# Paired head products, interleaved quarters in the scan, and low parts of the mixer's weights on VectorE in a two-layer hybrid encoder

## The chip, the cores and the metric

One core of a Trainium2 chip runs the whole program. The metric is device microseconds of one execution, the median of three runs. Engine names are those of the profile: PE is TensorE, DVE is VectorE, ACT is ScalarE, POOL is GpSimd, SP issues the DMAs.

## The reference, cut to what matters

Two residual layers over 512 positions of 1024 channels, in float32. Each layer is a mixer (three token mixers side by side, gated and summed, then an output projection) and a feed-forward with a convolution.

```python
h = rms_norm(x, attn_norm[l])
(qa, ka, va, qs, ks_, vs, qkv_c, z_c, beta_c, a_c, gate_c) = jnp.split(h @ w_in[l], splits, axis=-1)
# n: neighbourhood attention, 4 heads; s: sliding window, 8 query heads on 2 key heads
# g: bidirectional gated delta net, 4 heads of 64, chunks of 64 positions, both directions:
lower = where(strict, (k*beta) @ k.T * decay, 0)      # per head and chunk, 64x64
u, w  = solve(lower + I, [v*beta, k*beta*exp(g)])
qk    = (q @ k.T) * decay
def step(S, xs):                                      # over the 8 chunks, one after the other
    v_new = u_c - w_c @ S
    o_c   = q_c @ S + qk_c @ v_new
    S     = S * d_c + k_c.T @ v_new
merged = g_na*(y_na @ w_branch_na[l]) + g_swa*(y_swa @ w_branch_swa[l]) + g_gdn*(y_gdn @ w_branch_gdn[l])
x = x + merged @ w_out[l]
u = depthwise_conv_centred(rms_norm(x, ffn_norm[l]) @ w_up[l], ffn_conv_w[l]) + ffn_conv_b[l]
a, b = jnp.split(u, 2, axis=-1)
x = x + (silu(a) * b) @ w_down[l]
```

## The kernel before, in words

Channels lie on the partitions and the 512 positions along a row, so a tile of activations is 128x512. All weights come as chunks of 1024x128 from one array, in a fixed numbering: 0 to 51 are projections, gates and branch weights of the mixer, 52 to 59 the output projection, 60 to 103 the up-projection (`CH_UP = 60`), 104 to 127 the down-projection. `load_w` fetches a chunk in halves of 128x512. A dense product in float32 is made of three products in a rounded format: ACT copies a half to its rounded high part (`wh`, line 142), POOL subtracts that from the raw half and writes the low part (`wl`, line 144), and `mm3` (lines 150 to 152) issues high x high, high x low and low x high, each 128x128 weights by 512 columns. There are three buffers each of raw, high and low halves, and six accumulators `mm` in PSUM. A layer has 256 halves, 120 of them in chunks below 60, and 3024 dense products.

The mixer is a list of steps (`ORDER`). Those of the delta net are, in turn: gates and projections (`gg`, `gp`), `gdn_cross` (products of keys with keys and queries for each head, with decays), `gdn_solve` (31 steps of elimination on DVE, lines 713 and 715, then transposes, lines 722 to 728, and small products on PE from line 749 on), `gdn_mid` (lines 783 to 815), `gdn_scan` (eight chunks, forward on partitions 0 to 63 and backward on 64 to 127) and `gdn_out` (from line 872). The delta net has three PSUM banks (`gd`). The attention steps `na` and `sa` (lines 415 to 540) and the gates of the merge lie beside them. In a step of the scan PE multiplies the state by `wn` (line 832), DVE adds the product to `VN` (835), PE multiplies `VN` by `kT` (843), DVE adds that to the decayed state `SA` (848).

A scheduler orders the instructions of each engine before the program runs, from its own estimate of times; each engine then works through its list strictly in turn and waits on semaphores. So a change of one line moves instructions all over the lists.

Of the kernel before, what the change touches and what calls it, by code (L numbers as in the profile page):

```python
# [7 lines left out]
F32 = mybir.dt.float32  # L8
# [27 lines left out]
CH_UP = 60  # L36
# [25 lines left out]
def encoder_kernel(ctx, tc, xT, wall, par, cst, nab, out, depth=2, dbg=None):  # L62
# [70 lines left out]
    def load_w(l, c, nk=8):  # L133
# [3 lines left out]
        for o in range(0, nk, 4):  # L137
# [6 lines left out]
            G.tensor_tensor(lo[:, :n], raw[:, :n], hi.bitcast(F32)[:, :n], op=ALU.subtract)  # L144
# [130 lines left out]
    for l in range(depth):  # L275
# [374 lines left out]
        def gdn_cross():  # L650
            line[0] = "g"
            nonlocal Q, Qu, Xo, Xg, Lt, Rt, kds, qdec

            Q, Qu = by2("Q")
            Xo, Xg, Lt = (big(F32, (128, 32, 32), name=n) for n in ("Xo", "Xg", "Lt"))
            kds = [[doubled(kq[j][i][:, :, 0, :]) for i in range(2)] for j in range(2)]
            qdec = pair(name="qd") + pair(name="qd")
            for hh in range(4):
                j, rr = hh // 2, slice(64 * (hh % 2), 64 * (hh % 2) + 64)
                pe, pr = decay_sums(hh, (msr, blk))  # L660
                eg = tmp(name="eg")
                S.activation(out=eg, in_=pr, func=AF.Exp)
                for d in range(2):
                    r = slice(64 * d, 64 * d + 64)
                    for i in range(2):
                        ns = slice(4 * i, 4 * i + 4)
                        V.tensor_tensor(n8(qdec[hh])[r, ns], n8(eg)[r, ns], kq[j][i][rr, :, 1, :], op=ALU.mult)  # L667
                T.matmul(pe, lhsT=idb, rhs=nmb.unsqueeze(1).to_broadcast([128, 8, 64]), start=False, stop=True)
                e = tmp(name="E")
                S.activation(out=e, in_=pe, func=AF.Exp)  # L670
                on("ebk", "V").tensor_tensor(n8(e), n8(e), bc(bk, hh, 0, 8), op=ALU.mult)
                xt = tmp(name="X")
                for n0 in (0, 4):
                    kd = kds[j][n0 // 4]
                    pk = bank("gd")
                    for n in range(4):
                        T.matmul(pk[:, 128 * n:128 * n + 128], lhsT=kd[rr, n].rearrange("p d i -> p (d i)"),
                                 rhs=kq[j][n0 // 4][rr, n].rearrange("p c i -> p (c i)"), start=True, stop=True)
                    pkv = pk.rearrange("p (n c i) -> p c n i", n=4, c=2)
                    en = n8(e)[:, n0:n0 + 4]  # L680
                    V.tensor_tensor(n8(xt)[:, n0:n0 + 4], pkv[:, 0], en, op=ALU.mult)
                    V.tensor_tensor(Qu[n0 // 4 * 2 + hh // 2][:, :, hh % 2], pkv[:, 1], en, op=ALU.mult)

                for q4 in range(4):
                    r = slice(32 * q4, 32 * q4 + 32)
                    o = 32 * (q4 % 2)
                    cpx = (S.activation if q4 % 2 else G.tensor_copy)(
                        out=Xg[r].rearrange("p i (h n) -> p h n i", h=4)[:, hh], in_=n8(xt)[r, :, o:o + 32], **({"func": AF.Copy} if q4 % 2 else {}))
                    if q4 == 2:
                        lastg[0] = cpx  # L690
                    if q4 in (0, 3):
                        S.activation(out=Xo[r, 8 * hh:8 * hh + 8], in_=n8(xt)[r, :, 32 - o:64 - o], func=AF.Copy)
            Rt = big(F32, (128, 32, 32), "Rt")
# [123 lines left out]
        def gdn_scan():  # L817
# [7 lines left out]
            for s in range(8):  # L825
                ns = (s, 7 - s)
                half = [slice(0, 64), slice(64, 128)]
                if s:
                    pv = bank("gd", (128, 4, 64))
                    for d, r in enumerate(half):  # L830
                        for hh in range(4):
# [4 lines left out]
                if s < 7:  # L836
                    pd = bank("gd", (128, 4, 64))
                    sd = tmp(shape=(128, 8, 64), name="sd")[:, 0:4]
                    for d, r in enumerate(half):
                        if s:  # L840
                            G.tensor_tensor(sd[r], SA(ns[d])[r], hn(dec[:, 64:96])[r, :, ns[d]].unsqueeze(2).to_broadcast([64, 4, 64]), op=ALU.mult)
                        for hh in range(4):
# [289 lines left out]
```

## Time and profile before

| | us |
|---|---|
| median of 3 runs | 1711.9 (1708.8 to 1712.89) |
| the profiled execution | 1711.75 |
| its span, first to last instruction | 1710.0 |
| mean granted TensorE clock, share of full | 0.986 |
| PE busy | 1656.6 |
| POOL in line 144 | 683.8 in 512 instructions |

The profile is read in stretches of time from the start of the span. In the first layer the mixer runs up to about 521 us, and the first product of the solve stands at 259 us; the feed-forward ends at about 895 us. The second layer repeats this from 895 us, with the first product of its solve at 1105 us and its feed-forward from about 1366 us. A busy PE in these rows can include products that only wait in the pipe, so the number of products in a stretch is read beside the busy time.

### The profile page before, as it was taken

The page shows a single profiled execution, that of the slowest core. Times are in us where ns is not written, and L with a number is a line of the kernel's source. Part 1 is how long each engine was busy: PE and PEld are TensorE (multiplying, and loading weights), DVE is VectorE, ACT ScalarE, POOL GpSimd, SP SyncE. Part 2 cuts the span into 40 slices and gives each one's busy share as a digit, 9 for nine tenths or more (in the row PEclk, how much of TensorE's full clock was granted, in tenths as well). Part 3 has the DMA queues.
Part 4 walks back from the last instruction along what each step waited for, and adds up shares of the span by engine and source line. Part 5 has one row for each costly group of instructions (what it writes and reads, how often), then busy time and mean ns, then how long its engine had stood idle before and what let it go on. Part 6 is the DMA issues. An engine that isn't in the chain of part 4 may idle for free.

```text
span 1710.0 us, 25217 instructions
## 1 busy us (share of the span) xinstructions
PE 1656.6 (97%) x9196; PEld 1319.6 (77%) x9196; DVE 1008.1 (59%) x1809; ACT 739.1 (43%) x1436; POOL 834.5 (49%) x752
## 2 busy tenths in 40 slices
PE   7989999999999999999999998899999999999999
PEld 5766767777888888878886776777878888888887
DVE  5489996534547777741125898955255487777200
ACT  5445545423445444443334555554234354444321
POOL 4665442264544555544448554422644545555543
PEclk9989999999999999999999999999999999999999
DMA  5222211122452332234333221110324523222432
GB/s 205 74 64 76 70 62 45 38 69 73 132 190 87 99 99 96 96 115 132 114 104 94 67 72 56 56 44 26 99 91 138 178 87 99 93 93 92 136 121 70
DMA packets 91500, 160.46 MB, mean 94 GB/s; under 512 B 10352, under 2 KB 17136, under 8 KB 91376
## 3 DMA queue, kind: packets, MB, share of 16 engines
q1 hardware_dynamic: 91376, 158.85, 28.9%
q8 instruction: 72, 1.18, 0.3%
q14 instruction: 52, 0.43, 0.1%
HBM read 147.80 MB, written 8.39 MB: 91 GB/s over the span
## 4 chain that ended last, share of the span: by engine, by line
PE 79%; DVE 14%; issue 3%; ACT 2%; DMA 1%; POOL 0%; SPq 0%; DVEq 0%; ACTq 0%; POOLq 0%
PE mm L152 23%; PE mm L150 23%; PE mm L151 23%; DVE Rt L715 1%; DVE Tm L713 1%; PE at L535 1%; PE at L531 1%; DVE qd L667 1%; DVE lg L428 1%; DVE fix L172 1%; PE gd L843 1%; PE gd L832 1%; DVE fix L170 1%; PE gd L812 1%; PE at L509 1%
## 5 line engine op out<-in xcount | busy, mean ns | idle before, releaser
L144 POOL TENSOR_TENSOR wl<-wr,wh 128x512 fp32r<-128x512 f32 (+1 forms) x512 | 683.8, 1344 | 792.2 <-ACT wh L142 739.1
L150 PE MATMUL mm<-hh,wh 128*128 128x512 f32 x1408 | 560.2, 398 | 15.3 <-ACT wh L142 13.1
L152 PE MATMUL mm<-hh,wl 128*128 128x512 f32 x1408 | 559.3, 399 | 1.8 <-POOL wl L144 1.7
L151 PE MATMUL mm<-hl,wh 128*128 128x512 f32 x1408 | 556.0, 395 | 0.1
L142 ACT ACTIVATE wh<-wr 128x512 fp32r<-128x512 f32 (+1 forms) x512 | 312.4, 617 | 354.7 <-PE mm L151 213.0
L150 PEld LDWEIGHTS mm<-hh,wh 128*128 128x128 f32 x1408 | 268.0, 190 | 74.2 <-ACT wh L142 15.9
L152 PEld LDWEIGHTS mm<-hh,wl 128*128 128x128 f32 x1408 | 267.7, 190 | 65.1 <-POOL wl L144 6.2
L151 PEld LDWEIGHTS mm<-hl,wh 128*128 128x128 f32 x1408 | 267.7, 190 | 58.3 <-issue 1.9
L234 DVE SCALAR_TENSOR_TENSOR cv<-up,fix,cv 128x511 f32<-128x511 f32 x88 | 142.0, 1613 | 2.8
L233 DVE SCALAR_TENSOR_TENSOR cv<-up,fix,cv 128x511 f32<-128x511 f32 x88 | 85.9, 977 | 88.5 <-ACT cv L232 88.5
L152 PE MATMUL mm<-act,wl 128*128 128x512 f32 x352 | 137.2, 390 | 0.6 <-POOL wl L144 0.6
L150 PE MATMUL mm<-act,wh 128*128 128x512 f32 x352 | 137.1, 389 | 0.3 <-ACT wh L142 0.3
L151 PE MATMUL mm<-act,wh 128*128 128x512 f32 x352 | 137.0, 389 | 0.0
L971 DVE TENSOR_TENSOR xo<-xo,mm 128x512 f32<-128x512 f32 x16 | 11.0, 687 | 192.3 <-PE mm L152 192.3
L232 ACT ACTIVATE cv<-up,fix 128x512 f32<-128x512 f32 x88 | 70.8, 809 | 34.7 <-DVE up L280 34.7
L162 ACT ACTIVATE act<-cv 128x512 fp32r<-128x512 f32 x44 | 27.8, 632 | 126.0 <-DVE cv L954 126.0
L152 PEld LDWEIGHTS mm<-act,wl 128*128 128x128 f32 x352 | 66.1, 188 | 15.3 <-POOL wl L144 1.3
L150 PEld LDWEIGHTS mm<-act,wh 128*128 128x128 f32 x352 | 66.1, 188 | 14.2 <-ACT wh L142 0.7
L151 PEld LDWEIGHTS mm<-act,wh 128*128 128x128 f32 x352 | 66.1, 188 | 13.7
L953 ACT ACTIVATE cv<-cv 128x512 f32<-128x512 f32 x44 | 27.8, 633 | 86.2 <-DVE cv L234 86.2
L280 DVE TENSOR_TENSOR up<-mm,rstd 128x512 f32<-128x512 f32 x88 | 59.5, 680 | 8.2 <-ACT rstd L228 8.2
L900 ACT ACTIVATE gt<-gt 128x512 f32<-128x512 f32 x48 | 30.2, 630 | 66.4 <-DVE gt L280 66.3
(285 smaller groups left out, 2228.5 us busy)
## 6 DMA issues: line engine op xcount, KB each, us to landing
wr<-in_wall_dram SPq DMA_DIRECT2D x496, 256.0 KB, 2.8
xs<-xo SPq DMA_DIRECT2D x24, 256.0 KB, 2.9
xo<-xs SPq DMA_DIRECT2D x24, 256.0 KB, 3.7
xo<-in_xT_dram SPq DMA_DIRECT2D x16, 256.0 KB, 4.9
sw<-raw SPq DMA_DIRECT2D x40, 64.0 KB, 2.0
wr<-in_wall_dram SPq DMA_DIRECT2D x16, 128.0 KB, 3.3
out_dram<-xo SPq DMA_DIRECT2D x8, 256.0 KB, 2.1
nab<-in_nab_dram SPq DMA_DIRECT2D x8, 248.0 KB, 2.8
```

The source lines that it names most:

```text
L142: S.activation(out=hi[:, :n], in_=raw[:, :n], func=AF.Copy)
L144: G.tensor_tensor(lo[:, :n], raw[:, :n], hi.bitcast(F32)[:, :n], op=ALU.subtract)
L150: T.matmul(acc, lhsT=wh, rhs=rh, start=start, stop=False)
L151: T.matmul(acc, lhsT=wh, rhs=rl, start=False, stop=False)
L152: T.matmul(acc, lhsT=wl, rhs=rh, start=False, stop=stop)
L162: S.activation(out=hi, in_=src, func=AF.Copy)
L232: S.activation(out=dst, in_=src, func=AF.Identity, scale=w[:, 1:2], bias=bias)
L233: V.scalar_tensor_tensor(dst[:, 1:L], src[:, 0:L - 1], w[:, 0:1], dst[:, 1:L], op0=ALU.mult, op1=ALU.add)
L234: V.scalar_tensor_tensor(dst[:, 0:L - 1], src[:, 1:L], w[:, 2:3], dst[:, 0:L - 1], op0=ALU.mult, op1=ALU.add)
L280: V.tensor_tensor(dst, acc, rstd, op=ALU.mult)
L900: S.activation(out=gt[q], in_=gt[q], func=AF.Tanh, scale=0.5)
L953: S.activation(out=cv[0], in_=cv[0], func=AF.Silu)
```

## The change: what it does

Three edits. Low parts of chunks below 60 (all weights in front of the feed-forward) are written by DVE instead of POOL. In `gdn_cross` two heads, which lie on partitions 0 to 63 and 64 to 127, go through the products of line 677 together, each into a bank of its own, and their products stand in turn; their copies follow after both. In `gdn_scan` the products stand in turn between the two directions, not four of one and then four of the other.

```diff
-            G.tensor_tensor(lo[:, :n], raw[:, :n], hi.bitcast(F32)[:, :n], op=ALU.subtract)
+            (G if c >= CH_UP else V).tensor_tensor(lo[:, :n], raw[:, :n], hi.bitcast(F32)[:, :n], op=ALU.subtract)
...
-            for hh in range(4):
-                j, rr = hh // 2, slice(64 * (hh % 2), 64 * (hh % 2) + 64)
+            for j in range(2):
+                es, xts = [], []
+                for e in range(2):
+                    hh, rr = 2 * j + e, slice(64 * e, 64 * e + 64)
...
                 for n0 in (0, 4):
                     kd = kds[j][n0 // 4]
-                    pk = bank("gd")
+                    pks = [bank("gd") for _ in range(2)]
                     for n in range(4):
-                        T.matmul(pk[:, 128 * n:128 * n + 128], lhsT=kd[rr, n].rearrange("p d i -> p (d i)"),
-                                 rhs=kq[j][n0 // 4][rr, n].rearrange("p c i -> p (c i)"), start=True, stop=True)
...
+                        for e in range(2):
+                            rr = slice(64 * e, 64 * e + 64)
+                            T.matmul(pks[e][:, 128 * n:128 * n + 128], lhsT=kd[rr, n].rearrange("p d i -> p (d i)"),
+                                     rhs=kq[j][n0 // 4][rr, n].rearrange("p c i -> p (c i)"), start=True, stop=True)
...
                     pv = bank("gd", (128, 4, 64))
-                    for d, r in enumerate(half):
-                        for hh in range(4):
+                    for hh in range(4):
+                        for d, r in enumerate(half):
                             T.matmul(pv[r, hh], lhsT=n8(wn[hh])[r, ns[d]], rhs=SA(ns[d])[r, hh], start=True, stop=True,
...
-                        for hh in range(4):
+                    for hh in range(4):
+                        for d, r in enumerate(half):
                             T.matmul(pd[r, hh], lhsT=kT(ns[d], hh)[r], rhs=VN(ns[d])[r, hh], start=True, stop=True,
```

Lines after the edits move by 6 to 10: 677 becomes 683, 713 and 715 become 722 and 724, 749 becomes 758, 832 becomes 841, 843 becomes 852. This text uses the numbers of before.

On PE, in the first step of the first layer's scan, the four products of the forward state stand before the four of the backward state:

```order
L832 MATMUL gd_2946<-SA_2928,wn_564_2736 64x64
L832 MATMUL gd_2946<-SA_2928,wn_565_2737 64x64
L832 MATMUL gd_2946<-SA_2928,wn_566_2738 64x64
L832 MATMUL gd_2946<-SA_2928,wn_567_2739 64x64
L832 MATMUL gd_2946<-SA_2931,wn_564_2736 64x64
L832 MATMUL gd_2946<-SA_2931,wn_565_2737 64x64
L832 MATMUL gd_2946<-SA_2931,wn_566_2738 64x64
L832 MATMUL gd_2946<-SA_2931,wn_567_2739 64x64
```

Now they stand in turn (`SA_2928` is the forward state, `SA_2931` the backward one):

```order
L841 MATMUL gd_2946<-SA_2928,wn_564_2736 64x64
L841 MATMUL gd_2946<-SA_2931,wn_564_2736 64x64
L841 MATMUL gd_2946<-SA_2928,wn_565_2737 64x64
L841 MATMUL gd_2946<-SA_2931,wn_565_2737 64x64
L841 MATMUL gd_2946<-SA_2928,wn_566_2738 64x64
L841 MATMUL gd_2946<-SA_2931,wn_566_2738 64x64
L841 MATMUL gd_2946<-SA_2928,wn_567_2739 64x64
L841 MATMUL gd_2946<-SA_2931,wn_567_2739 64x64
```

The eight products are the same; what moved is their turn.

On DVE, in the middle of the elimination of the first layer (`Tm` and `Rt` are its two instructions), there stood only work of the merge beside the chain:

```order
L713 TENSOR_TENSOR Tm_2424<-Lt_2158,Rt_2335 128x252
L715 TENSOR_TENSOR Rt_2335<-Rt_2335,Tm_2424 128x18x14
L713 TENSOR_TENSOR Tm_2424<-Lt_2158,Rt_2335 128x255
L715 TENSOR_TENSOR Rt_2335<-Rt_2335,Tm_2424 128x17x15
L912 SCALAR_TENSOR_TENSOR ma_651_3323<-gt_635_3243,mm_3337 128x512
L912 SCALAR_TENSOR_TENSOR ma_652_3324<-gt_636_3244,mm_3345 128x512
L713 TENSOR_TENSOR Tm_2424<-Lt_2158,Rt_2335 128x256
L912 SCALAR_TENSOR_TENSOR ma_677_3433<-gt_661_3353,mm_3435 128x512
L715 TENSOR_TENSOR Rt_2335<-Rt_2335,Tm_2424 128x16x16
```

Now low parts (`wl`) and instructions of the neighbourhood attention (lines 422 to 428) stand in it:

```order
L144 TENSOR_TENSOR wl_3457<-wr_3453,wh_3455 128x512
L722 TENSOR_TENSOR Tm_2424<-Lt_2158,Rt_2335 128x255
L422 ISA lg_1277,fix<-at_1284,nab_1275,fix 128x192
L422 ISA fix 128x1
L724 TENSOR_TENSOR Rt_2335<-Rt_2335,Tm_2424 128x17x15
L722 TENSOR_TENSOR Tm_2424<-Lt_2158,Rt_2335 128x256
L426 RECIPROCAL fix<-fix 128x2
L724 TENSOR_TENSOR Rt_2335<-Rt_2335,Tm_2424 128x16x16
L428 TENSOR_SCALAR lg_1277<-lg_1277,fix 128x192 x2
L722 TENSOR_TENSOR Tm_2424<-Lt_2158,Rt_2335 128x255
L724 TENSOR_TENSOR Rt_2335<-Rt_2335,Tm_2424 128x15x17
```

Ahead of the last transpose of the solve DVE has 61 low parts more than before in the first layer and 62 in the second; its other work ahead of that place is the same.

On PE, around the first product of the first layer's solve, sliding-window attention (lines 509 to 535) and branch products stood directly ahead of it, and both groups of 32 stood together:

```order
L535 MATMUL at_1751<-th_1766,sv_335 64x256 x2
L509 MATMUL at_1799<-kdh_61_284,qs_101_464 128x384
L510 MATMUL at_1799<-kdl_63_286,qs_101_464 128x384
L535 MATMUL at_1751<-th_1775,sv_335 64x256 x2
L509 MATMUL at_1804<-kdh_62_285,qs_102_465 128x384
L510 MATMUL at_1804<-kdl_64_287,qs_102_465 128x384
L749 MATMUL gd_2556<-WT_2525,Xo_2156 32x32 x32
L749 MATMUL gd_2591<-WT_2525,Xo_2156 32x32 x32
L152 MATMUL mm_3614<-hh_85,wl_3606 128x512
```

Now dense products of the gates stand ahead, and the groups are cut up:

```order
L152 MATMUL mm_3673<-hh_131,wl_3665 128x512
L150 MATMUL mm_3673<-hh_142,wh_3669 128x512
L151 MATMUL mm_3673<-hl_143,wh_3669 128x512
L531 MATMUL at_1752<-fix,spr_1736 128x128
L531 MATMUL at_1752<-fix,spr_1723 128x128
L531 MATMUL at_1752<-fix,spr_1741 128x128
L150 MATMUL mm_3712<-hh_85,wh_3702 128x512
L151 MATMUL mm_3712<-hl_86,wh_3702 128x512
L758 MATMUL gd_2556<-WT_2525,Xo_2156 32x32
L758 MATMUL gd_2591<-WT_2525,Xo_2156 32x32
L758 MATMUL gd_2556<-WT_2525,Xo_2156 32x32 x21
```

What moved: ahead of this product stand 736 dense products of the layer where 692 stood, with 8 products of line 531, 6 of line 535 and 8 of lines 509 and 510 fewer; in the second layer 758 where 692 stood, with the same attention. Between it and the scan stand 82 dense products in the first layer and 70 in the second where 126 stood, and in the scan 81 and 92 where 147 stood. Of the products of line 683 about half stand in turn; for the others the second bank comes free later and four of one head stand together.

## Rows read from the trace of the kernel before

**Rows 1.** The page, its parts 1, 2 and 4: shares, PE in forty slices, the chain by engine.

```profile
PE 1656.6 (97%) x9196; PEld 1319.6 (77%) x9196; DVE 1008.1 (59%) x1809; ACT 739.1 (43%) x1436; POOL 834.5 (49%) x752
...
PE   7989999999999999999999998899999999999999
...
PE 79%; DVE 14%; issue 3%; ACT 2%; DMA 1%; POOL 0%; SPq 0%; DVEq 0%; ACTq 0%; POOLq 0%
```

**Rows 2.** Busy time by stretch; each engine with its instructions, TensorE clock, DMA share, GB/s.

```profile
60.00:259.00 199.00, 180.20 (x950) 134.76 (x948) 175.14 (x380) 103.51 (x231) 113.39 (x138) 0.96 0.24 73
...
259.00:277.00 18.00, 17.97 (x307) 13.88 (x308) 9.92 (x35) 11.19 (x30) 2.94 (x3) 0.81 0.15 46
...
330.00:384.00 54.00, 53.88 (x402) 41.85 (x402) 21.86 (x54) 16.25 (x34) 32.80 (x34) 1.00 0.20 65
...
570.00:600.00 30.00, 30.00 (x134) 24.83 (x133) 21.26 (x23) 13.61 (x23) 15.77 (x12) 1.00 0.30 93
...
895.00:960.00 65.00, 57.91 (x307) 43.37 (x306) 42.64 (x86) 28.94 (x57) 45.05 (x34) 0.89 0.27 82
...
960.00:1105.00 145.00, 133.33 (x709) 102.04 (x707) 133.70 (x305) 80.06 (x186) 76.22 (x107) 0.99 0.20 64
...
1123.00:1176.00 53.00, 53.00 (x499) 40.63 (x498) 29.09 (x88) 27.23 (x71) 10.00 (x8) 1.00 0.11 36
```

**Rows 3.** Busy time by stretch, of line 144 (low parts on POOL) alone; same columns.

```profile
60.00:259.00 199.00, 57.80 (x43) 0.96 0.24 73
...
895.00:1105.00 210.00, 65.17 (x47) 0.96 0.22 70
```

**Rows 4.** Timeline of DVE, 217 to 226: start, duration, engine, line, operation, tiles, shape, count.

```profile
217.83 0.42 DVE L715 TENSOR_TENSOR Rt<-Rt,Tm 128x252 f32<-128x252 f32 x1
...
218.36 1.40 DVE L713 TENSOR_TENSOR Tm<-Lt,Rt 128x255 f32<-128x255 f32 x1
...
219.79 1.40 DVE L715 TENSOR_TENSOR Rt<-Rt,Tm 128x255 f32<-128x255 f32 x1
...
223.76 1.48 DVE L713 TENSOR_TENSOR Tm<-Lt,Rt 128x255 f32<-128x255 f32 x1
```

**Rows 5.** Timeline of POOL, the same stretch.

```profile
218.18 4.17 POOL L144 TENSOR_TENSOR wl<-wr,wh 128x512 fp32r<-128x512 f32 x3 [4.39 <-PE mm L152]
...
223.68 1.29 POOL L144 TENSOR_TENSOR wl<-wr,wh 128x512 fp32r<-128x512 f32 x1 [1.33 <-ACT wh L142]
```

**Rows 6.** Instructions of one line (163, then 234): durations in ns, least, median, most.

```profile
L163 DVE TENSOR_TENSOR act<-cv,act x44: 677/692/694, 533.1 to 1595.7; 128x512 fp32r<-128x512 f32 x44
...
L234 DVE SCALAR_TENSOR_TENSOR cv<-up,fix,cv x88: 737/1661/1777, 525.3 to 1592.6; 128x511 f32<-128x511 f32 x88
```

**Rows 7.** Timeline of PE in the scan: 343 to 346.

```profile
343.70 0.96 PE L832 MATMUL gd<-SA,wn 64*64 64x64 f32 x16
...
344.60 0.65 PE L535 MATMUL at<-th,sv 128*64 128x256 f32 x4
...
345.18 1.13 PE L843 MATMUL gd<-VN,kT 64*64 64x64 f32 x16
```

**Rows 8.** Timeline of PE in the middle step, 286 to 288.

```profile
286.72 1.38 PE L794 MATMUL gd<-W,kE 64*64 64x64 f32 x40
```

**Rows 9.** Timeline of PE in the head products, 1010 to 1012.

```profile
1010.40 1.16 PE L677 MATMUL gd<-kq,dup 64*128 64x128 f32 x8
...
1011.49 0.50 PE L150 MATMUL mm<-hh,wh 128*128 128x512 f32 x1
```

**Rows 10.** Timeline of PE, 246 to 264, up to the first solve product.

```profile
246.77 0.93 PE L531 MATMUL at<-fix,spr 128*128 128x128 f32 x7
...
259.03 3.81 PE L749 MATMUL gd<-WT,Xo 32*32 32x32 f32 x128 [2.72 <-DVE fix L513]
```

**Rows 11.** Groups of instructions by line: busy, mean ns, idle before and its releaser.

```profile
L835 DVE TENSOR_TENSOR VN<-gd,VN 64x256 f32<-64x256 f32 x28 | 11.8, 423 | 22.9 <-PE gd L832 22.5
...
L152 PE MATMUL mm<-hh,wl 128*128 128x512 f32 x1408 | 559.3, 399 | 1.8 <-POOL wl L144 1.7
```

More of the change, by code (lines that the diff above doesn't have):

```diff
@@ L657, in gdn_cross @@
             qdec = pair(name="qd") + pair(name="qd")
-            for hh in range(4):
-                j, rr = hh // 2, slice(64 * (hh % 2), 64 * (hh % 2) + 64)
[L660 to L672, printed above, removed]
+            for j in range(2):
+                es, xts = [], []
+                for e in range(2):
+                    hh, rr = 2 * j + e, slice(64 * e, 64 * e + 64)
+                    pe, pr = decay_sums(hh, (msr, blk))
+                    eg = tmp(name="eg")
+                    S.activation(out=eg, in_=pr, func=AF.Exp)
+                    for d in range(2):
+                        r = slice(64 * d, 64 * d + 64)
+                        for i in range(2):
+                            ns = slice(4 * i, 4 * i + 4)
+                            V.tensor_tensor(n8(qdec[hh])[r, ns], n8(eg)[r, ns], kq[j][i][rr, :, 1, :], op=ALU.mult)
+                    T.matmul(pe, lhsT=idb, rhs=nmb.unsqueeze(1).to_broadcast([128, 8, 64]), start=False, stop=True)
+                    ex = tmp(name="E")
+                    S.activation(out=ex, in_=pe, func=AF.Exp)
+                    on("ebk", "V").tensor_tensor(n8(ex), n8(ex), bc(bk, hh, 0, 8), op=ALU.mult)
+                    es.append(ex)
+                    xts.append(tmp(name="X"))
@@ L673, in gdn_cross @@
                 for n0 in (0, 4):
                     kd = kds[j][n0 // 4]
-                    pk = bank("gd")
+                    pks = [bank("gd") for _ in range(2)]
                     for n in range(4):
-                        T.matmul(pk[:, 128 * n:128 * n + 128], lhsT=kd[rr, n].rearrange("p d i -> p (d i)"),
-                                 rhs=kq[j][n0 // 4][rr, n].rearrange("p c i -> p (c i)"), start=True, stop=True)
-                    pkv = pk.rearrange("p (n c i) -> p c n i", n=4, c=2)
@@ L680, in gdn_cross @@
[L680 to L692, printed above, removed]
+                        for e in range(2):
+                            rr = slice(64 * e, 64 * e + 64)
+                            T.matmul(pks[e][:, 128 * n:128 * n + 128], lhsT=kd[rr, n].rearrange("p d i -> p (d i)"),
+                                     rhs=kq[j][n0 // 4][rr, n].rearrange("p c i -> p (c i)"), start=True, stop=True)
@@ new lines, in gdn_cross @@
+                    for e in range(2):
+                        pkv = pks[e].rearrange("p (n c i) -> p c n i", n=4, c=2)
+                        en = n8(es[e])[:, n0:n0 + 4]
+                        V.tensor_tensor(n8(xts[e])[:, n0:n0 + 4], pkv[:, 0], en, op=ALU.mult)
+                        V.tensor_tensor(Qu[n0 // 4 * 2 + j][:, :, e], pkv[:, 1], en, op=ALU.mult)
+                for e in range(2):
+                    hh = 2 * j + e
+                    for q4 in range(4):
+                        r = slice(32 * q4, 32 * q4 + 32)
+                        o = 32 * (q4 % 2)
+                        cpx = (S.activation if q4 % 2 else G.tensor_copy)(
+                            out=Xg[r].rearrange("p i (h n) -> p h n i", h=4)[:, hh], in_=n8(xts[e])[r, :, o:o + 32], **({"func": AF.Copy} if q4 % 2 else {}))
+                        if q4 == 2:
+                            lastg[0] = cpx
+                        if q4 in (0, 3):
+                            S.activation(out=Xo[r, 8 * hh:8 * hh + 8], in_=n8(xts[e])[r, :, 32 - o:64 - o], func=AF.Copy)
```

## The prediction

> **What bounds the kernel now.** First the page: PE is busy for 97% of the span and holds 79% of the chain that ended last, DVE holds 14% of it [rows 1]. So time is won by less work on PE, or where PE is short of work. The forty slices show where that is: PE falls to 8 or 9 tenths only near the start and around slice 22, where the layers begin [rows 1]. The stretches say it sharper [rows 2]. In the feed-forward 134 dense products go through in 30.0 us, 0.224 us each, with PE full; nothing in the change touches that. From 60 us to the solve of the first layer at 259 us PE is busy for 180.2 of 199 us at a clock of 0.96, while DVE is busy for 175.1. In the second layer, from 895 to 1105 us, PE misses 7.1 and 11.7 us, and from 960 us on DVE is busy for 133.7 of 145. So ahead of the solve DVE sets the pace, and PE has about 19 us of idle time in each layer besides a lower clock. The product that opens the solve came after 2.72 us of idle PE, released by DVE [rows 10]; behind it the granted clock of the stretch is 0.81, that is some time at the lower of its two levels (1.2 and 2.4 GHz) [rows 2]. From there to the end of the layer PE is full: 53.00 of 53 us ahead of the scan in the second layer, 53.88 of 54 in the first one's scan [rows 2]. The end of a layer is therefore the start of its solve plus the PE work behind that.
>
> **Scan in turn: 8.1 us less on PE.** Sixteen records (eight products, two passes each) of line 832 take 0.96 us, four products of one quarter at a time [rows 7]. Line 794 already stands in turn between the same two quarters: 40 records in 1.38 us, so with 0.22 us for the last one 1.16/39 = 0.030 us from one to the next [rows 8]. Sixteen then take 15 x 0.030 + 0.22 = 0.67 us, 0.29 us less; 14 batches in each of two layers give 28 x 0.29 = 8.1 us. But both halves now end together and DVE adds them one after the other (0.42 us each [rows 11]). The shortest half-step of before is 1.48 us from line 832 to 843, with 0.6 us of other work between [rows 7]. The new one can hardly be under 0.67 + 0.42 + 0.34 + 0.1, about 1.5 us. In the order of after five half-steps of a layer have between 0 and 1 us of other PE work between their batches, against four of 0.3 to 1.4 before; those five leave some 2 us of idle PE in a layer. I put back 4 us, with 0 and 12 as ends: the DVE queue has 7 or 8 low parts in a scan, and each can hold an add back by 0.7 us.
>
> **Head products in turn: nothing on the end.** Eight records of line 677 take 1.09 us to the next instruction [rows 9]. No row shows two tiles of 64 rows and 128 columns side by side: with nothing gained the 128 records cost what they do, with a full halving they would save 16 x 0.5 = 8 us, and since only half of them stand in turn in the order, 4 us. They stand ahead of the solve, where DVE sets the pace, so I count 0; the ends are -4 and +2 (a second bank of three is taken, and a head's decay sums wait for it).
>
> The Trainium skill (TensorEngine Tiling (Array Packing), Theoretical Speedup) gives up to twice the rate where the contraction has at most 64 rows. By it, as an estimate, the half that stands in turn would save those 4 us of PE work; the trace agrees for 64x64 quarters and shows nothing for 64x128, and the sum stays as it is.
>
> **Low parts on DVE: what they cost it.** 240 of 512 low parts move, 120 in a layer. An operation of this form with two inputs in SBUF takes 0.69 us on DVE [rows 6]. In 60 to 259 us 43 low parts ran on POOL, in 895 to 1105 us 47 [rows 3]; on DVE they are 43 x 0.69 = 30 us and 47 x 0.69 = 32 us. Against that stands what they cost DVE from POOL. Steps of the elimination take 0.42 us; the three that met a low part on POOL took 1.40, 1.40 and 1.48 us [rows 4, 5]. Four low parts there cost DVE 3.0 us, 0.76 each. The same is seen in the feed-forward, where line 234 has 0.74 us at least and 1.66 us in the middle [rows 6]. At 0.76 each 43 and 47 low parts give back 33 and 36 us. So the start of a solve lies between 4 us earlier (all low parts met such an operation) and 32 us later (none did). I take 0, nearest to the stretch that shows it; what is moved also has a cover in DVE's first 60 us and at 895 to 960 us, where DVE is busy for 42.6 of 65 [rows 2].
>
> The trace shows the two engines in each other's way there [rows 4, 5]. The Trainium skill (GPSIMD Engine Reference, Key points) has a rule for it that speaks against the change: GpSimd shares its interfaces to SBUF with VectorE, for VectorE operations with two SBUF inputs among others, and the new low parts are such operations. What that would do here is rival 4.
>
> **PE work moved ahead of the solve: 20 us.** With the solve at the same time, the 44 and 66 dense products that now stand ahead of it no longer stand behind it: 9.9 and 14.8 us at 0.224 us [rows 2]. In the first layer attention goes the other way: eight products of line 531 (16 records at 0.93/7 us [rows 10], 2.1 us), six of line 535 (0.65 us for four records [rows 7], 1.9 us), eight of 509 and 510 at some 0.15 us, together 5 us. Net 4.9 and 14.8 us. This fits into the 19 us that PE idles in front of each solve. The ends are 0 (PE idles behind the solve instead) and 20.
>
> **Two costs of the new order.** Behind the solve of the second layer 70 dense products fill the chain up to the scan where 126 did, 12.5 us less filler in 53 us that were full [rows 2]; I take 4 us of new idle time there, between 0 and 10. And a low part now waits in DVE's queue behind adds and evictions that wait for PE. Until now PE waited 1.7 us in all for low parts [rows 11]. In the order, most low parts have 6 to 10 us of PE work between the last product that DVE must wait for and their first use, but some 15 of 240 have under 2.7 us; at a quarter of a microsecond each that is 4 us, between 0 and 15. The output projection is covered: there a chunk's two low parts stand a whole chunk ahead.
>
> **Sum.** The profiled execution took 1711.75 us (span 1710.0 and 1.75 around it), the median of the runs is 1711.9, so no correction is needed. 1711.75 - 8.1 + 4 + 0 + 0 - 19.7 + 4 + 4 = 1696.
>
> **Rivals.**
> 1. VectorE holds the solve back (slower). Its place is the queue of DVE from 60 to 259 and 960 to 1105 us, full to 88 and 92%. If a low part gives back only a quarter of what it costs, each solve starts 0.69 - 0.19 = 0.5 us later per low part, 22 and 24 us, and PE has nothing to fill that with: 1696 + 46 less some 16 us that the early stretches cover = 1726. It decides from 8 us of delay a layer on. For it: DVE is the fullest engine there, and operations that read PSUM were not stretched by POOL. Against it: the measured 1.4 us steps, in the very chain that ends last.
> 2. The moved work gives nothing back (no change). PE idles in the scan and the middle step for what it did earlier; of the sum only the quarters remain: 1711.75 - 8.1 + 4 + 4 = 1712 down to 1708. For it: five empty half-steps and the thinner filler. Against it: the 53 us ahead of the second scan hold only 29.1 us of DVE work and 10.0 us of POOL work [rows 2], so the chain there has room.
> 3. The solve starts early and the clock stays up. With 0.76 us given back, less waiting of POOL's own work (tables of the attention, rope) behind low parts, and no idle PE in front of the solve, each solve comes 8 us sooner: 1696 - 16 = 1680.
> 4. The moved low parts meet what POOL keeps. That is 113.4 - 57.8 = 55.6 us of other work in 60 to 259 us, 28% of the stretch [rows 2, 3]. If 8 of the 61 low parts ahead of a solve meet it at 1.0 us each (1.4 against 0.42 us [rows 4]), each solve comes 8 us later: 1696 + 16 = 1712, no change.
> 5. The head products in turn don't overlap at all: +2 us of PE work, 1698, inside the forecast.
>
> **How the numbers follow.** A run of this kernel can't tell less than 0.3%, 5 us, from no change. Forecast (1684 to 1706) 0.46, early solve 0.12, head products without overlap 0.05: all faster, 0.63. No change, 1707 to 1717: 0.19, of it 0.06 by rival 4 and the rest by rival 2. Slower: 0.18, nearly all by rival 1. The likeliest case alone reaches from 1684 to 1707. The range for 8 in 10 goes from 1679, the middle of rival 3, to 1722, inside rival 1.
>
> **What would show it.** Right: batches of 832 and 843 at about 0.67 us; steps 713 and 715 back at 0.42 us; POOL's line 144 only in the feed-forward; the first product of each solve within 5 us of 259 us and 210 us after the layer's start, with more dense products ahead of it; idle PE in the scan under 3 us a layer. Wrong: DVE full and the solve late by over 8 us, or dense products of line 152 waiting for DVE by more than 10 us in all, or PE idle for over 10 us between solve and scan.

## The result and the profile after

The changed kernel takes 1687.3 us (median of 4 runs, 1684.6 to 1689.37) where the kernel before takes 1712.4 us on the same chip (4 runs, 1708.8 to 1715.77). The ratio is 0.9853 with an interval from 0.9826 to 0.988, so it is faster by 1.2 to 1.7%. The forecast was 1696 us. The profiled execution took 1689.37 us, with a span of 1687.3. Line numbers below are those of the changed kernel, unless a kernel is named whose products stand as before.

The page, parts 1, 2 and 4, answers to [rows 1]:

```profile
PE 1645.3 (98%) x9196; PEld 1313.4 (78%) x9196; DVE 1062.9 (63%) x2049; ACT 740.4 (44%) x1436; POOL 530.7 (31%) x512
...
PE   7999999999999999999999998999999999999999
...
PE 89%; DVE 5%; issue 2%; POOL 1%; ACT 1%; DMA 1%; SPq 0%; POOLq 0%; DVEq 0%; ACTq 0%
```

DVE does 240 more instructions and holds 5% of the chain instead of 14%. The stretches are cut at the same places of the work as in [rows 2]: up to the solve, to the scan, and the scan, first layer and then second (columns as there):

```profile
60.00:245.00 185.00, 175.25 (x970) 134.09 (x968) 167.14 (x423) 104.23 (x234) 59.53 (x94) 0.99 0.25 77
245.00:309.00 64.00, 61.44 (x753) 47.03 (x754) 38.91 (x111) 32.11 (x84) 0.00 (x0) 0.89 0.11 35
309.00:357.00 48.00, 44.89 (x369) 32.14 (x367) 30.46 (x79) 17.44 (x41) 15.46 (x18) 0.93 0.14 43
884.00:1095.00 211.00, 202.14 (x1075) 155.52 (x1074) 180.22 (x449) 115.10 (x253) 60.02 (x94) 0.96 0.24 76
1095.00:1151.00 56.00, 54.99 (x733) 42.43 (x731) 35.53 (x106) 30.68 (x80) 1.39 (x2) 0.97 0.09 30
1151.00:1197.00 46.00, 43.80 (x355) 31.59 (x356) 29.86 (x77) 16.16 (x40) 13.56 (x15) 0.93 0.15 46
```

Ahead of the first solve PE now idles for 9.8 us instead of 18.8, ahead of the second for 8.9 instead of 18.8. Up to the first solve DVE holds 43 instructions more and yet is busy for less: 167.1 us against 175.1. The low parts on DVE alone, in those two stretches, answer to [rows 3]:

```profile
60.00:245.00 185.00, 32.11 (x43) 0.00 (x0) 0.99 0.25 77
884.00:1095.00 211.00, 36.42 (x50) 0.00 (x0) 0.96 0.24 76
```

So what DVE did besides them kept it busy for 40 us less in the first layer (175.1 + 32.1 - 167.1) and 32.5 us less in the second (176.3 + 36.4 - 180.2, with 176.3 the two rows of the second layer in [rows 2] added). DVE's instructions overlap a little at their ends, so such a difference of busy times is only rough. Added up instruction by instruction, each against the median of the same operation, tiles and shape in `all_lows` (a run below, in which POOL has little to do), the figures are 34 and 30 us: DVE's instructions that ran beside one of POOL were longer by 39.1 and 36.2 us in all ahead of the two solves, and are now longer by 7.9 and 8.4 us, of which 2.7 and 2.4 us fall on the new low parts. Those that ran beside none were no longer before, nor are they now. The elimination is only 8 and 3 us of this, but it shows it best. In the timeline of DVE that answers to [rows 4], POOL now has no instruction from 195 to 216 us:

```profile
200.50 0.41 DVE L724 TENSOR_TENSOR Rt<-Rt,Tm 128x252 f32<-128x252 f32 x1
...
201.16 0.69 DVE L144 TENSOR_TENSOR wl<-wr,wh 128x512 fp32r<-128x512 f32 x1
201.76 0.42 DVE L722 TENSOR_TENSOR Tm<-Lt,Rt 128x255 f32<-128x255 f32 x1
...
202.44 0.42 DVE L724 TENSOR_TENSOR Rt<-Rt,Tm 128x255 f32<-128x255 f32 x1
```

No step takes 1.4 us any more; the longest of the 62 steps of each line is 0.43 us. The first products of the two solves, in the timeline of PE, answer to [rows 10]:

```profile
245.00 0.39 PE L758 MATMUL gd<-WT,Xo 32*32 32x32 f32 x4 [2.33 <-DVE WT L735]
246.28 1.45 PE L758 MATMUL gd<-WT,Xo 32*32 32x32 f32 x42 [0.88 <-DVE WT L737]
...
1095.57 3.80 PE L758 MATMUL gd<-WT,Xo 32*32 32x32 f32 x128
```

Each layer is then followed from its own start, which for the second is its first dense product. Before, that stands at 861.8 us, and not at 895 us, where the opening has the second layer begin; after, it stands at 850.4 us:

| us | first layer, before | after | second, before | after |
|---|---|---|---|---|
| start of the layer to the solve | 259.0 | 245.0 | 243.2 | 245.2 |
| solve to scan | 70.8 | 64.5 | 70.8 | 55.5 |
| scan | 54.0 | 47.5 | 54.0 | 46.3 |
| end of the scan to the end | 477.9 | 493.4 | 480.2 | 490.1 |
| sum | 861.8 | 850.4 | 848.2 | 837.1 |

Both layers gain 11 us, the first by an earlier solve, the second by less work behind a solve that comes 2 us later. Over whole layers, PE idles for 4.3 us less in the first (26.3 instead of 30.6) and 7.1 us less in the second (15.7 instead of 22.8), and is busy for 7.1 and 4.2 us less. It is at the lower clock for as long as before: about 24 us in the first layer in both kernels, 27 instead of 24 us in the second.

In the scan, in the timeline of PE, a batch in turn takes 0.68 us where it took 0.96 us in [rows 7], if both of DVE's adds are done. Eight of the 28 batches hold a wait of 0.34 to 0.42 us and take 1.1 us or more: DVE adds the two directions one after the other, and the batch starts behind the first add and goes on behind the second. The longest, 1.51 us, is at the lower clock besides. PE also waits ahead of some batches:

```profile
319.25 0.68 PE L841 MATMUL gd<-SA,wn 64*64 64x64 f32 x16
...
321.20 1.14 PE L853 MATMUL gd<-VN,kT 64*64 64x64 f32 x16 [0.52 <-DVE VN L844]
...
329.66 0.68 PE L853 MATMUL gd<-VN,kT 64*64 64x64 f32 x16
331.03 0.33 PE L841 MATMUL gd<-SA,wn 64*64 64x64 f32 x2 [0.69 <-DVE SA L858]
...
333.80 1.51 PE L853 MATMUL gd<-VN,kT 64*64 64x64 f32 x16
```

The two adds ahead of the batch at 321.20 us, in the timeline of DVE; its third record starts at 321.66 us:

```profile
320.73 0.88 DVE L844 TENSOR_TENSOR VN<-gd,VN 64x256 f32<-64x256 f32 x2
```

The windows behind the start of the first solve and around the long batch show PE's clock at its lower level, a granted clock of 0.50 (1.2 GHz). Ahead of the first stretch PE had idled for 2.33 us, ahead of the second for 0.2 to 0.7 us at several places:

```profile
245.60:259.20 13.60, 12.92 (x151) 9.55 (x152) 4.77 (x9) 5.15 (x10) 0.00 (x0) 0.50 0.19 60
...
334.40:337.80 3.40, 3.40 (x30) 2.19 (x30) 0.84 (x2) 0.29 (x1) 1.23 (x2) 0.50 0.00 0
```

Last, what PE waited for low parts, among the groups by line, answers to [rows 11]:

```profile
L152 PE MATMUL mm<-hh,wl 128*128 128x512 f32 x1408 | 558.9, 397 | 7.6 <-DVE wl L144 7.6
```

### The profile page after: what moved, and what is told of

Same layout as the page of the kernel before. It is cut to its first block, busy times and chain, and to the rows that moved or that the text cites. A ratio compares the mean times of both kernels' runs of the same rounds, so it can differ in the third digit from the quotient of the medians.

```text
span 1687.3 us, 25138 instructions
## 1 busy us (share of the span) xinstructions
PE 1645.3 (98%) x9196; PEld 1313.4 (78%) x9196; DVE 1062.9 (63%) x2049; ACT 740.4 (44%) x1436; POOL 530.7 (31%) x512
## 4 chain that ended last, share of the span: by engine, by line
PE 89%; DVE 5%; issue 2%; POOL 1%; ACT 1%; DMA 1%; SPq 0%; POOLq 0%; DVEq 0%; ACTq 0%
PE mm L152 26%; PE mm L150 26%; PE mm L151 26%; PE at L535 1%; PE at L531 1%; PE at L509 1%; PE gd L683 1%; PE at L438 1%; PE gd L821 1%; DVE wl L144 1%; PE at L510 1%; PE gd L335 0%; PE gd L758 0%; PE gd L853 0%; PE gd L841 0%
## 5 line engine op out<-in xcount | busy, mean ns | idle before, releaser
L144 POOL TENSOR_TENSOR wl<-wr,wh 128x512 fp32r<-128x512 f32 (+1 forms) x272 | 362.0, 1342 | 542.2 <-ACT wh L142 531.0
L144 DVE TENSOR_TENSOR wl<-wr,wh 128x512 fp32r<-128x512 f32 x240 | 173.4, 726 | 69.8 <-ACT wh L142 64.2
L232 ACT ACTIVATE cv<-up,fix 128x512 f32<-128x512 f32 x88 | 70.8, 809 | 34.7 <-DVE up L280 34.7
L415 POOL TENSOR_SCALAR nab<-nab,fix 128x248 f32<-128x248 f32 (+2 forms) x32 | 34.6, 1095 | 121.3 <-DVE fix L397 50.4
L850 POOL TENSOR_TENSOR sd<-SA,fix 64x256 f32<-64x256 f32 x24 | 16.1, 671 | 161.8 <-DVE SA L860 124.5
```

The lines of the kernel that those rows point to most:

```text
L144: (G if c >= CH_UP else V).tensor_tensor(lo[:, :n], raw[:, :n], hi.bitcast(F32)[:, :n], op=ALU.subtract)
L232: S.activation(out=dst, in_=src, func=AF.Identity, scale=w[:, 1:2], bias=bias)
L415: on("nab", "G").tensor_scalar(bias[:, e, 0:w], bias[:, e, 0:w], irn[:, c0:c0 + 1], None, op0=ALU.mult)
```

## The experiments

Ratios are to the kernel before, run on the same chip beside each kernel. `lows`, `pairs_scan`, `no_pairs` and `no_scan` shared a chip, `pool_again`, `pool_clear`, `all_lows` and `gd4` another, `scan`, `pair_no_turn`, `relief` and `no_pairs_all` a third; its median on them was 1711.8, 1712.6 and 1711.4 us. The changed kernel itself ran beside the kernel before on its own, so it is compared with the others through the ratios.

### One edit, two edits

Low parts alone, on the kernel before (`lows`):

```diff
-            G.tensor_tensor(lo[:, :n], ...)
+            (G if c >= CH_UP else V).tensor_tensor(lo[:, :n], ...)
```

> Only the low parts of the chunks in front of the feed-forward move to VectorE; the products of gdn_cross and gdn_scan stand as before. Theory A (VectorE no longer waits for GpSimd in the stretch that it sets): most of the gain is here, 1694 to 1703 us, and steps of the elimination stay at 0.42 us. Theory B (the gain is the PE work saved by tiles that overlap): 1708 to 1716 us.

Measured: 1690.3 us, ratio 0.9878 [0.9839, 0.9916]. This one line carries 21 of the 25 us, more than its first theory had. Its solves stand at 247.6 us and 236.6 us after the start of the layer, 11 and 7 us sooner than before.

The two product edits without the low parts (`pairs_scan`), that is the changed kernel with line 144 as before:

> Both product edits, low parts all on GpSimd as before. Theory A: only the scan's 8 us of PE work less its stalls, 1702 to 1709 us, solve of the first layer still at 255 us or later. Theory B: 1688 to 1697 us.

Measured: 1716.6 us, ratio 1.0018 [0.9996, 1.004]: no gain, if anything a loss, and outside both theories.

The changed kernel with one head at a time again (`no_pairs`; `gdn_cross` as before, the other two edits kept):

> The changed kernel with gdn_cross as before (one head after the other). Theory A: these products lie where VectorE sets the pace, so 1685 to 1692 us, within 5 us of the changed kernel. Theory B (they save 4 to 7 us of PE work that counts): 1692 to 1697 us.

Measured: 1682.1 us (1681.68 to 1682.72), ratio 0.9825 [0.9792, 0.9858]. The best so far, and below both theories: each of its four runs is shorter than each of the four of the changed kernel.

The changed kernel with the scan as before (`no_scan`):

> The changed kernel with the scan's products in the old turn (four of one quarter, then four of the other). If the 0.29 us of each of the 28 batches count in full: 1695 us. If the scan's new waits for both halves take them back, as the 47.5 us scan of the changed kernel suggests (37 us of PE work): 1686 to 1690 us.

Measured: 1693.6 us, ratio 0.9892 [0.9858, 0.9925]: beside the other two edits the turn in the scan is worth 0.4%, 6 to 7 us.

The turn in the scan alone, low parts on POOL (`scan`; only the two loops of `gdn_scan` are changed in the kernel before):

```diff
-                    for d, r in enumerate(half):
-                        for hh in range(4):
+                    for hh in range(4):
+                        for d, r in enumerate(half):
```

> The kernel before with the scan's products in turn alone; all low parts stay on POOL, the head products stay one head at a time. Theory A (the turn saves PE work by itself, 28 batches at 0.29 us, and with DVE lightly used in the scan of this kernel the adds come at once): PE work about 8 us less and the time 8 us below the kernel before, 1704 (1701 to 1707). Theory B (the gain needs the filler or the early solve that the moved low parts bring; without them PE waits for the adds as long as it has won): 1709 to 1713. With the run of both product edits together, 1716.6, the difference is what the head products in turn cost with the low parts on POOL: by A 12 us, by B about 5.

Measured: 1704.2 us, ratio 0.9962 [0.9946, 0.9978], 7 us, as its first theory had it. So the turn gains the same with and without the moved low parts. The windows of its two scans show why nothing is lost there, with the filler of before still in place:

```profile
328.70:380.00 51.30, 50.69 (x402) 38.33 (x401) 21.62 (x55) 16.48 (x34) 32.67 (x34) 1.00 0.21 68
1168.20:1220.00 51.80, 51.27 (x394) 38.52 (x392) 22.46 (x56) 16.36 (x35) 32.63 (x32) 1.00 0.22 72
```

PE idles for 0.6 and 0.5 us at full clock, where the changed kernel idles for 3.1 and 2.2 us and drops to 0.93. From `scan` to `pairs_scan` the head products in turn cost 0.56% (1.0018 less 0.9962), about 10 us, with low parts on POOL; from `no_pairs` to the changed kernel 0.28%, about 5 us. The first of the two differences is clear of the noise, but not all of it is shown to be the head products' own: in the profile of `pairs_scan`, PE idles for 7.9 us more in the first layer than in that of `scan`, and 6.9 us of this are one wait for a low part at 22 us, far ahead of the head products.

### Is it POOL that stretches VectorE?

The trace of the kernel before shows it by itself. Of the 124 steps of the elimination, 96 ran beside no instruction of POOL, and each took as long as the same step in `all_lows`, within 0.02 us. The other 28 met a subtraction of POOL. Twelve of them were longer, by 0.1 to 1.1 us: each of these began while the subtraction ran and ended 0.08 to 0.28 us after it. The other sixteen were not longer: eleven had begun before the subtraction, and when the other five began, the one that ran had at most 0.12 us to go. The same holds for all of DVE: 957 instructions beside none of POOL's took no longer than in `all_lows`, and 852 beside one took 212 us longer in all, 96 us of it in the convolution of the feed-forward. None of the 260 among them that read PSUM was longer by more than 0.02 us.

The changed kernel in which POOL repeats each moved subtraction, in two halves, into a buffer that nobody reads (`pool_again`):

```diff
+            if c < CH_UP:
+                dl = wp.tile([128, 2, 128], BF16, tag="dl", name=nm("dl"), bufs=1)
+                for i in range(0, n, 2):
+                    G.tensor_tensor(dl, raw[:, i:i + 2], hi.bitcast(F32)[:, i:i + 2], op=ALU.subtract)
```

> The changed kernel, where GpSimd besides does every subtraction of the moved low parts once more, in two halves of 128x256, into a scratch tile that nothing reads. PE, VectorE and ScalarE have the work of the changed kernel; only GpSimd's traffic is back. Theory A (two-input operations of VectorE wait for GpSimd): the gain goes, 1705 to 1740 us, and steps of the elimination are again at 1.2 to 1.5 us in part. Theory C (what helped is that low parts come out of a faster engine and that GpSimd's own steps of the chain no longer queue behind them): these also queue again, so no verdict from the time alone, but steps stay at 0.42 us and VectorE's mean for a low part stays at 0.73 us.

Measured: 1753.3 us, ratio 1.0242 [1.0225, 1.0259]: 4% longer than the changed kernel, with not one instruction more on DVE. That is beyond theory A's range, and the steps are stretched less than it had (0.95 us at most), but they are stretched, as are the low parts, which theory C excluded. Its groups by line, low parts on DVE, their repetition on POOL, and the steps of the elimination:

```profile
L148 POOL TENSOR_TENSOR dl<-wr,wh 128x256 bf16<-128x256 f32 x480 | 444.9, 927 | 310.4 <-issue 146.0 <-ACT wh L142 111.2 <-POOL dl L148 25.5
...
L144 DVE TENSOR_TENSOR wl<-wr,wh 128x512 fp32r<-128x512 f32 x240 | 211.2, 884 | 63.8 <-ACT wh L142 61.6 <-PE mm L155 1.3 <-DVE qd L673 0.4
...
L726 DVE TENSOR_TENSOR Tm<-Lt,Rt 128x31 f32<-128x31 f32 (+15 forms) x62 | 24.5, 394 | 3.0 <-DVE Rt L728 0.5
```

One low part takes 884 ns on DVE instead of 726, a step 394 ns instead of 339, and DVE is busy for 1189.0 us instead of 1062.9. The pairing in time is plain in its timelines, DVE and then POOL:

```profile
226.61 0.75 DVE L144 TENSOR_TENSOR wl<-wr,wh 128x512 fp32r<-128x512 f32 x1
227.29 0.95 DVE L728 TENSOR_TENSOR Rt<-Rt,Tm 128x256 f32<-128x256 f32 x1
...
228.49 0.41 DVE L726 TENSOR_TENSOR Tm<-Lt,Rt 128x255 f32<-128x255 f32 x1
```

```profile
226.09 1.86 POOL L148 TENSOR_TENSOR dl<-wr,wh 128x256 bf16<-128x256 f32 x2 [3.42 <-ACT wh L142]
```

The step inside POOL's 1.86 us takes 0.95 us, the next one outside it 0.41. The run doesn't say how much of its 66 us is stretching alone: the repetition also holds the raw weights longer and stands in front of POOL's own work, and PE waits for low parts for 31.7 us instead of 7.6. Dummy work without these two was not tried.

The other explanation, that low parts were only waiting in POOL's queue, is put to the test on the kernel before by taking five other kinds of work off POOL and leaving all low parts on it (`pool_clear`):

```diff
-ENG = {}
+ENG = {"nab": "V", "cos": "V", "nql": "V", "ql": "V", "ma1": "V"}
```

> The kernel before with the low parts on GpSimd, but GpSimd's other larger work (bias tables, cosine products, low parts of the queries, one add of the merge: 82 instructions) on VectorE, so that nothing of the chain queues behind a low part. Theory A: VectorE gets fuller and still waits for GpSimd: 1712 us or more, up to 1735. Theory C (the queue of GpSimd was the cause): faster, 1695 to 1705 us.

Measured: 1713.1 us, ratio 1.001 [0.9999, 1.0021]. POOL is busy for 97 us less and nothing is won; the steps take 411 and 419 ns on average, as before (415 and 440). So a shorter queue does not end the stretching. The time alone decides less, for DVE has 82 instructions more and is busy for 32 us more, which can hide a gain. But the queue of the kernel before held nothing up that the end depends on: POOL has 0% of the chain that ended last [rows 1], and PE waited for low parts for 1.7 us in all [rows 11].

All 512 low parts on DVE (`all_lows`):

```diff
-            (G if c >= CH_UP else V).tensor_tensor(lo[:, :n], ...)
+            V.tensor_tensor(lo[:, :n], ...)
```

> The changed kernel with the low parts of the feed-forward on VectorE too. PE is full there, so both theories expect the time of the changed kernel, 1684 to 1691 us. Theory A besides: line 234 falls from 1.61 us to about 0.75, so that VectorE's busy time in the feed-forward hardly rises although it has 272 more operations.

Measured: 1686.2 us, ratio 0.9846 [0.983, 0.9863], no difference to the changed kernel that can be told. But the convolution of the feed-forward, line 234 of [rows 6], shows the same effect once more; first the changed kernel, then `all_lows` (ns, least, median, most):

```profile
L234 DVE SCALAR_TENSOR_TENSOR cv<-up,fix,cv x88: 737/1662/1778, 513.7 to 1569.9; 128x511 f32<-128x511 f32 x88
```

```profile
L234 DVE SCALAR_TENSOR_TENSOR cv<-up,fix,cv x88: 740/751/753, 515.3 to 1563.9; 128x511 f32<-128x511 f32 x88
```

With POOL quiet none of the 88 takes over 0.76 us. It gains no time because PE is full there, as [rows 2] showed.

### What the pairs cost

A fourth bank for the delta net (`gd4`), on the changed kernel:

```diff
-NB |= {"mm": 6, "gd": 3, "at": 5, ...}
+NB |= {"mm": 6, "gd": 4, "at": 5, ...}
```

> The changed kernel with four PSUM banks of the delta net's kind instead of three. If the pairs start the solve late (it comes 5 to 9 us later in the second layer than in the kernel without them) because the second pair of banks comes free late: all head products stand in turn, 1680 to 1684 us. If it is the order of the work on VectorE: 1686 us or more.

Measured: 1688.0 us, ratio 0.986 [0.9845, 0.9874], no gain. Whether more turn would help stays open: the order still puts only 27 pairs of the 128 records in turn, as in the changed kernel. But the first solve now stands at 241.3 us and the second 236.8 us after the start of its layer, 3.7 and 8.4 us sooner than in the changed kernel and for the second as early as in `no_pairs`, and still the time is that of the changed kernel. So an earlier solve alone does not give the 5 us back.

Two heads together, but four products of one head and then four of the other in the program (`pair_no_turn`):

```diff
-                    for n in range(4):
-                        for e in range(2):
-                            rr = slice(64 * e, 64 * e + 64)
+                    for e in range(2):
+                        rr = slice(64 * e, 64 * e + 64)
+                        for n in range(4):
```

> The changed kernel in which the two heads still go together, each into a bank of its own, with their copies behind both, but the four products of one head stand before the four of the other. Undoing the pairs altogether gave 1682.1 against 1687.3. Theory A (two heads' decays, evictions and copies in one block hold the solve back, whatever the turn of the products): the time stays above 1686, at 1687 to 1692, the first product of the second layer's solve at 243 us or later after the layer's start, and PE work 2 to 4 us more than in the changed kernel. Theory B (the turn itself does it, since both banks are then held until the last product): 1680 to 1684, the solve at 236 to 239 us as without pairs.

Measured: 1689.7 us, ratio 0.9872 [0.9843, 0.9902]; the first solve at 241.3 us, the second 247.8 us after the start of the layer. The time is theory A's: without the turn inside the block nothing is won, so it is not the turn that costs. The test is not quite clean, for the scheduler put 16 pairs of records in turn by itself. What the block does to the head products shows in the second layer. In `no_pairs`, a head's decay `E` is scaled by DVE and its eight products follow (timelines of DVE and PE, joined here in two fences):

```profile
965.68 0.69 DVE L671 TENSOR_TENSOR E<-E,fix 128x512 f32<-128x512 f32 x1
...
981.26 0.69 DVE L671 TENSOR_TENSOR E<-E,fix 128x512 f32<-128x512 f32 x1 [1.65 <-ACT E L670]
```

```profile
969.97 1.16 PE L677 MATMUL gd<-kq,dup 64*128 64x128 f32 x8
```

In the changed kernel, the same two views:

```profile
974.27 0.68 DVE L673 TENSOR_TENSOR E<-E,fix 128x512 f32<-128x512 f32 x1
...
984.70 0.68 DVE L673 TENSOR_TENSOR E<-E,fix 128x512 f32<-128x512 f32 x1
```

```profile
988.04 0.71 PE L683 MATMUL gd<-kq,dup 64*128 64x128 f32 x4
```

The first head's `E` is ready at 975 us, but its products stand behind the second head's, ready at 985. The head products begin 137.6 us after the start of the layer instead of 124.8, and the solve 245.2 instead of 236.8. But this wait is not what costs the 5 us, for PE does not stand idle for it: ahead of that solve it idles for 8.9 us in the changed kernel and for 8.5 us in `no_pairs`. The 8.4 us are 24 dense products more (5.4 us) and 10 us more at the lower clock (5 us), less 2 us that the head products save. Over both layers, PE idles for 4.9 us more in the changed kernel (42.0 against 37.1), all of it in the first layer, and is at the lower clock for 10 us more (51 against 41, which costs 5 us); the head products give 4.1 us back. The sum, 5.9 us, is nearly the 6.6 us between the two profiles. By line, what idles more is PE's wait for low parts, 7.6 us against 1.3. Why the order around the pairs brings the low parts late, no run shows.

### Two tries to do better

`no_pairs` with twelve copies of the attentions' keys taken from DVE to ACT (`relief`):

```diff
-ENG = {}
+ENG = {"nkh": "S", "kdh": "S"}
```

> The changed kernel with one head at a time again (1682.1), and the copies of the two attentions' keys to their rounded high parts (nkh, kdh) on ACT instead of DVE: 8 at 0.675 and 4 at 1.17 us, some 5 us of DVE a layer, all ahead of the solve. Theory A (DVE sets the pace ahead of the solve): each solve 2 to 3 us earlier and 1676 to 1680. Theory B (with POOL out of the way DVE is no longer the bound there, PE and the chain of the delta net are): 1681 to 1684, the solves within 1 us of 247.7 and 236.8 us.

Measured: 1686.1 us, ratio 0.985 [0.9825, 0.9875]. No gain over `no_pairs`: it is 4 us longer, outside both theories. The second solve comes 3 us sooner (233.7 us), the first 6 us later (253.3). The scheduler's new order moves the solves by as much as the copies on DVE were worth, so whether DVE still sets the pace there stays open.

`no_pairs` with all low parts on DVE (`no_pairs_all`; the edit of `all_lows` on top):

> The changed kernel with one head at a time again (1682.1), and all 512 low parts on DVE, those of the feed-forward too. In the changed kernel the same step brought DVE's convolution from 1.6 us an instruction to 0.75 and the time from 1687.3 to 1686.2, no difference that can be told. Theory A (PE is full in the feed-forward, so a free DVE there is worth nothing): 1680 to 1684. Theory B (the layers' borders, where PE waits for the last sums of the feed-forward, get shorter with unstretched DVE operations): 1676 to 1680.

Measured: 1680.8 us (1679.87 to 1682.2), ratio 0.9825 [0.9797, 0.9853]. Equal to `no_pairs` as far as this can be told. In every run these two are shorter than both kernels of this case, though the intervals of their ratios overlap that of the changed kernel.

## Why the prediction was right, and where it was not

The sign, the place and the order of size were right: 1687.3 us lies in the range and in the likeliest case's own, 9 us under 1696. Of the signs that were named, the first solve's place missed: it stands 14 us early, not within 5 us of 259. Split by layers, the forecast's terms come to -5 us in the first (-4.9 - 4 + 2 + 2) and -11 in the second (-14.8 - 4 + 2 + 4 + 2). The table shows -11.4 and -11.1. So the error is in the first layer: there PE idles for 4.3 us less where the terms come to 0.9, and is busy for 7.1 us less where they come to 4. That the second layer fits is in part luck, for its terms missed both ways: the scan cost more than was taken, the filler less.

**Low parts, start of the solve: this step failed in the first layer.** "I take 0" was put against -14.0 and +2.0 us. The price of a low part was nearly right (0.75 and 0.73 us by the stretches, 0.69 taken), and so was what comes back, 34 and 30 us against 33 and 36. What failed is the step from there to the solve. DVE's stretch ahead of the first solve got 14 us shorter: 2 us by cost and return, 6 us because its instructions overlap more, and 6 us in which it had stood idle. The sum had a term for the first alone. On PE's side it left out what rival 3 had: the clock. Before, PE ran at the lower level for 17 us ahead of the first solve, now for 3.4 us (a granted clock of 0.96 and 0.99 in the stretch), which is worth 6.8 us of time; ahead of the second solve it is 17 us in both (0.96 and 0.96). The end has none of these 6.8 us, for behind the first solve, up to the end of the scan, the clock takes as much again. With 9.0 us less idle time and 4.9 us more work ahead of the solve, and 2 us of the head products' saving, this gives 4.9 - 9.0 - 6.8 - 2 = -13. Without the pairs the solves come 11.3 and 6.4 us sooner than before, so that rival 3 (8 us each, 1680) is near what the other two edits do by themselves, at 1682.1.

The Trainium skill (GPSIMD Engine Reference, Key points) says that GpSimd shares its interfaces to SBUF with VectorE, with contention for VectorE operations of two SBUF inputs among others. The traces agree: 0.42 against 1.40 us before [rows 4], 0.41 against 0.95 in `pool_again`, 0.75 against 1.66 in the feed-forward. The prediction quoted it as speaking against the change; it spoke for it, since it also prices what POOL did until then. Rival 4, which rested on it, fell: 94 instructions of POOL are left ahead of each solve, but the 12 and 13 low parts that meet one there lose 2.7 and 2.4 us where the rival had 8, and a low part on DVE takes 0.685 us at the median.

**Moved work.** It went where the step said. Idle PE ahead of the solves fell by 9.0 and 9.9 us, 18.9 in all against 19.7 counted. That the sums agree is luck in part, for the terms were 4.9 and 14.8. Rival 1 fell (DVE is not later by 22 us) and rival 2 fell.

**Scan in turn.** 0.68 us against 0.67 forecast for a batch, and 7 us for the edit alone: right. The 4 us put back for stalls were too few, and put to the wrong edit. PE idles for 3.1 and 2.2 us in the two scans, and 6.8 us at the lower clock in each cost 3.4 more: 12 us, the outer end of the 0 to 12. But `lows` and `no_scan`, with the scan's products as before and only the filler thinner, lose at least as much: PE idles for 1.5 to 2.8 us in each of their scans, at a granted clock of 0.86 to 0.93, while `scan`, with the turn and the filler of before, idles for 0.6 and 0.5 us at full clock. So what is missing is the filler that went ahead of the solve. Nor do low parts hold DVE's adds back in the rows, as the upper end had it: ahead of the adds stand evictions and attention.

**Filler between solve and scan.** 4 us were taken for the second layer. It idles for 1.0 us there. The first layer, for which nothing was taken, idles for 2.6 us and is 6.8 us longer at the lower clock, 3.4 us more.

**Late low parts.** PE waits 7.6 us for them, 5.9 more than before, against 4. With one head at a time it is 1.3 us (`no_pairs`), so they are late with the order around the pairs.

**Head products.** "I count 0" with an upper end of +2. On PE the optimistic end came true: line 683 is busy for 14.4 us instead of 18.2, and rival 5 fell. On the end it was +5, outside the bounds: with the pairs come 4.9 us of idle PE in the first layer, about what PE waits longer for low parts, and 5 us by the lower clock, and the sum priced only banks and products. That a head's products wait for the other head's decay is plain in the rows, but it is not shown to cost the end anything. The Trainium skill (TensorEngine Tiling (Array Packing), Theoretical Speedup) gives up to twice the rate there, and the trace agrees for the 27 pairs of records that stand in turn.

## What to carry to other kernels

An instruction's price on one engine includes what it does to another's: before counting a move as so many times its new duration, look for operations of the receiving engine that are longer whenever the giving engine works, and count those as returned. Where PE waits, count its idle time and its time at the lower clock together, over the whole kernel: here PE idled for 11 us less and the clock gave nothing back, since PE was at the lower clock for as long as before, only elsewhere. And an edit that saves work on one engine can lose more by the order that it brings: the pairs saved 4 us of PE's work and cost 10 us of waiting and clock.

## What the runs showed of the hardware that was not expected

Two products of 64 rows by 128 columns, on the two halves of the partitions and each into its own bank, start 3 to 14 ns apart in the 27 pairs of records that stand in turn, and the next two mostly 112 ns after the first, which is what one record takes when it stands alone (111 to 112 ns from start to start). Which of the two begins first decides whether POOL's subtraction stretches a step of the elimination: of those that began before it none was longer. And how far it is stretched goes with POOL's own instruction: beside subtractions of 128x512 the longest took 1.48 and 1.49 us, beside those of 128x256 into a 16-bit format 0.77 and 0.95 us, against 0.43 us with neither.
